# First token tile of a two-layer hybrid trunk: other order, queues and engines for its loads, squares and splits, and the forget columns projected in another chunk

## The chip, the cores and the metric

The kernel runs on one core of one Trainium2 chip. The metric is the device time of one launch in microseconds (us), median of several runs. The core's engines appear in the profile as PE (matmul) and PEld (its weight loads), DVE, ACT, POOL and SP; SP issues DMAs, and so can ACT.

## The reference, cut to what matters

Two layers; in each, an RMS norm, one input projection whose columns go to three token mixers, and an output projection with a second RMS norm and the residual.

```python
h = _rms_norm(x, pre_g)
z = jnp.einsum('bsd,de->bse', h, w_in)          # 2048 x 1024 by 1024 x 3846, float32
a_z, r_z, f_z = jnp.split(z, [A_COLS, A_COLS + R_COLS], axis=-1)
...                                              # a: gelu, spatial gating; r: retention
f_q, f_k, f_v, f_g, f_lg = jnp.split(f_z, [F_WIDTH, 2 * F_WIDTH, 3 * F_WIDTH, 4 * F_WIDTH], axis=-1)
cum_f = jnp.cumsum(jax.nn.log_sigmoid(f_lg + b_f), axis=1)     # 6 forget columns
logits = q k^T * scale + cum_f[q] - cum_f[k]                   # causal softmax, then times v
...
o = jnp.einsum('bse,ed->bsd', y, w_out)
return x + _rms_norm(o, post_g)
```

## The kernel before, in words

Tokens are worked in 16 tiles of 128 (`t`), the 1024 input dimensions in 8 slices of 128 (`k`). Every float32 operand of a large matmul is split into a high part H (an ACT cast to float32r, L175) and a low part L (the difference, on DVE or POOL, L177); a product is three matmuls, H·H, H·L and L·H (L489 to L491 in the chunks that are computed token by token).

`in_proj` takes the 3846 columns in chunks, in this order: `v` (384 value columns and the 6 forget columns, 390 in all), then `g`, `q`, `k` (computed transposed, L266 to L268), then `a0`, `a1` (384 columns each), then `r0`, `r1`, `r2` (512 each). Within a chunk the loop runs over `t`, and within `t` over `k`. At one `k` of tile `t` the operands of tile `t + 1` are split (`token_split`), and `weight_gen` loads and splits the weights of the next chunk. The result `z` of a tile alternates between two PSUM banks.

What follows a tile (`v_post`, `a_post`, `r_post`, `norm`) is a generator on a background list. `bg.add` runs it to its first `yield`; `bg.tick()` after every `k` advances each by one `yield`, and `wait(n)` yields n times. So these numbers are the program's order: every engine executes its instructions in the order in which the code emits them.

`v_post` adds the bias to the 6 forget columns (`lg`, L289). After the last tile of `v` it runs `cum_forget`: Abs, Exp and Ln on ACT, then 16 ticks later a transpose and a running sum (`cs`), 4 ticks later an offset, a split into `cH` and `cL`, and twelve small stores from SP (L322). `r_post` makes `at` (scores times decay, L374) on DVE, which two matmuls read (L379, L380). `e1`, `lt`, `cH`, `cL`, `at` and the `uv` of `a_post` all come from one pool tag with two buffers:

```python
e1 = tp.tile([P, 96], F32, name="e1", tag="at")
cH = tp.tile([96, P], F32R, name="cH", tag="at")
cL = tp.tile([96, P], F32R, name="cL", tag="at")
at = tp.tile([P, 2, P], F32, name="at", tag="at")
```

A tile of this tag can be written once everything that reads the tile two before it is done, DMAs included. DMAs signal on eight lanes in turn, so one is issued once the eighth before it has landed.

At the start of the program 30 transposes of an identity (`warm`, L909) keep PE busy. The first token tile is loaded whole on SP, then the gain, two weight slices, the second token tile, and so on; each weight slice is two DMAs (384 and 6 columns). Its norm is Square on ACT, three small POOL operations, and a product on DVE (`h`, L155); eight transposes go to PSUM (`pt`, L161), a copy to `hT` (L162), and the split from `hT`.

At the end, `last_tile` computes the last 128 tokens' output in two halves of 512 columns, each with a Square, then three POOL operations (L827 to L829), and per half a DVE operation and a store.

Of the kernel before, what the change touches and what calls it, by code (L numbers as in the profile page):

```python
# [12 lines left out]
AF = mybir.ActivationFunctionType  # L13
# [63 lines left out]
def trunk(ctx, tc, a, out):  # L77
# [13 lines left out]
    def U(name, dt=F32):  # L91
        return up.tile([P, 1024], dt, name=name, tag="u")
# [35 lines left out]
    def load_gain(src):  # L128
        t = U("gain")
        nc.sync.dma_start(out=t, in_=src.partition_broadcast(P))  # L130
        return t

    def load_x(src):
        x = U("x")
        nc.sync.dma_start(out=x, in_=src)
        return x
# [64 lines left out]
    def token_half(hT, t, g):  # L201
        return split(hT[t // 4][:, 4 * g:4 * g + 4, (t % 4) * P:(t % 4 + 1) * P])
# [4 lines left out]
    def in_proj(l, hT, w0, cur, next_norm):  # L207
# [1 line left out]
        w_in = a["w_in"][l].rearrange("(k p) e -> k p e", p=P)  # L209
        rz = w_in[:, :, 768:2304].rearrange("k p (c e) -> k p c e", c=4)  # L210
        az = w_in[:, :, 0:768].rearrange("k p (c e) -> k p c e", c=3)
        chunks = [("v", [(w_in[:, :, 3072:3456], 384), (w_in[:, :, 3840:3846], 6)]),
                  ("g", [(w_in[:, :, 3456:3840], 384)]),
                  ("q", [(w_in[:, :, 2304:2688], 384)]), ("k", [(w_in[:, :, 2688:3072], 384)])]
        chunks += [(("a", m), [(az[:, :, :, m * P:(m + 1) * P], 384)]) for m in range(2)]
        chunks += [(("r", m), [(rz[:, :, :, m * P:(m + 1) * P], 512)]) for m in range(3)]
        W = [w0] + [[] for _ in chunks[1:]]

# [77 lines left out]
        def cum_forget():
# [129 lines left out]
        def a_post(m, t, z):  # L426
            s, r = divmod(t, 4)
            if r == 0:
                state["vu"] = U("vu")
            vn, ug = (state["vu"][:, i * 512:(i + 1) * 512].rearrange("p (e r d) -> p e r d", e=2, r=4) for i in range(2))  # L430
            uv = tp.tile([P, 256], F32, name="uv", tag="at")
            nc.scalar.activation(out=uv, in_=z[:, 0:256], func=AF.Gelu_apprx_tanh)
            th = tp.tile([P, P], F32, name="rth", tag="rth")
            nc.scalar.activation(out=th, in_=z[:, 256:384], func=AF.Tanh, scale=0.5)
            g = tp.tile([P, P], F32, name="rg", tag="rg")
            nc.vector.scalar_tensor_tensor(out=g, in0=th, scalar=1.0, in1=z[:, 256:384], op0=ALU.add, op1=ALU.mult)
            nc.gpsimd.tensor_tensor(out=ug[:, :, r], in0=heads(uv[:, 0:P]), in1=heads(g), op=ALU.mult)
            mv = small("mv", [P, 2, 2])
            for e in range(2):
                bs = small("bs", [P, 6])  # L440
                nc.vector.bn_stats(out=bs, in_=uv[:, P + e * HD:P + (e + 1) * HD])
                nc.vector.bn_aggr(out=mv[:, e], in_=bs)
            hr = small("hr", [P, 2])
            nc.gpsimd.tensor_scalar(out=hr, in0=mv[:, :, 1], scalar1=EPS, scalar2=None, op0=ALU.add)
            nc.gpsimd.tensor_tensor(out=hr, in0=hr, in1=mhalf, op=ALU.pow)
            yield from wait(3)
            for e in range(2):
                nc.vector.tensor_scalar(out=vn[:, e, r], in0=uv[:, P + e * HD:P + (e + 1) * HD],
                                        scalar1=mv[:, e, 0:1], scalar2=hr[:, e:e + 1],
                                        op0=ALU.subtract, op1=ALU.mult)  # L450
# [15 lines left out]
            nc.sync.dma_start(out=y[s][0][:, m * P:(m + 1) * P].rearrange("(r p) c -> p r c", p=P),
                              in_=ya.rearrange("p (r c) -> p r c", r=4))
# [3 lines left out]
        for ci in (0, 4, 5, 6, 7, 8):  # L471
# [6 lines left out]
            for t in range(NT):  # L478
# [6 lines left out]
                for k in range(KT):  # L485
                    H, L = cur[k // 4]
                    wH, wL = W[ci][k]
                    c = slice((k % 4) * P, (k % 4 + 1) * P)
                    mm(z[:, :n], lhsT=H[:, c], rhs=wH[:, :n], start=(k == 0), stop=False)  # L489
                    mm(z[:, :n], lhsT=H[:, c], rhs=wL[:, :n], start=False, stop=False)  # L490
                    mm(z[:, :n], lhsT=L[:, c], rhs=wH[:, :n], start=False, stop=(k == KT - 1))  # L491
                    if ci == 0 and t == NT - 1:
                        nxt.append(split(hT[0][:, k]))
                    elif k == (5 if ci == 0 and next_norm else 0) and not (last and t == NT - 1):
                        nxt = token_split(hT, (t + 1) % NT)
                    bg.tick()
                    if last and k % 4 == 3:
                        loads.issue()
                    if fx and k % 2 and fx.chunks < PRE and t >= 10:
                        fx.s_step()  # L500
                        loads.issue()
                        fx.e_step()
                    if last and t == NT - 1 and k in TK:
                        fx.l_step()
                        fx.t_step()
# [267 lines left out]
    def out_proj(l, y, W, og, x_src, x_dst, hT, next_w, ahead):  # L773
# [33 lines left out]
        def last_tile(cur):  # L807
# [8 lines left out]
            for g in range(2):  # L816
                oo = bank("oo", "S")
                for k in range(KT):
# [3 lines left out]
                    for xx, i, first, last in ((H, 0, True, False), (H, 1, False, False), (L, 0, False, True)):  # L822
                        mm(oo, lhsT=xx[:, c], rhs=w[i], start=(k == 0 and first), stop=(k == KT - 1 and last))  # L823
                    bg.tick()
                nc.scalar.activation(out=junk[:, cs[g]], in_=oo, func=AF.Square, accum_out=ss[:, g:g + 1])  # L825
                nc.vector.tensor_tensor(out=o[:, cs[g]], in0=oo, in1=post[:, cs[g]], op=ALU.mult)
            nc.gpsimd.tensor_tensor(out=rs, in0=ss[:, 0:1], in1=ss[:, 1:2], op=ALU.add)  # L827
            nc.gpsimd.tensor_scalar(out=rs, in0=rs, scalar1=1.0 / DM, scalar2=EPS, op0=ALU.mult, op1=ALU.add)  # L828
            nc.gpsimd.tensor_tensor(out=rs, in0=rs, in1=mhalf[:, 0:1], op=ALU.pow)  # L829
            for c in cs:  # L830
                nc.vector.scalar_tensor_tensor(out=o[:, c], in0=o[:, c], scalar=rs, in1=x[:, c], op0=ALU.mult, op1=ALU.add)  # L831
                nc.sync.dma_start(out=x_dst(t)[:, c], in_=o[:, c])

        ys = load_y(0)
        yield
# [41 lines left out]
        if hT is None:  # L877
# [3 lines left out]
    x_src = lambda t: a["x"][t * P:(t + 1) * P, :]  # L881
    hT = [big_tile(f"hT{b}") for b in range(4)]
    W0 = []
    first_w = lambda l: [(a["w_in"][l].rearrange("(k p) e -> k p e", p=P)[:, :, 3072:3456], 384),
                         (a["w_in"][l].rearrange("(k p) e -> k p e", p=P)[:, :, 3840:3846], 6)]
    xq = {}

    def tables_in():
# [14 lines left out]
        if t + 2 < NT:  # L903
            bg.add(norm(xq.pop(t + 2), pg, hT, t + 2, 10, "B"))

    wg = weight_gen(first_w(0), W0, lambda k: k % 3 > 0)
    xq[0] = load_x(x_src(0))
    for _ in range(WU):
        nc.tensor.transpose(bank("warm", "B")[:, 0:P], ident, ident)  # L909
    pg = load_gain(a["pre_gain"][0])  # L910
    next(wg)
    next(wg)
    xq[1] = load_x(x_src(1))
    first = norm(xq.pop(0), pg, hT, 0, 1, "B", (slice(0, 512), slice(512, DM)))
    next(first)
    next(wg)
    next(wg)
    cur = []
    next(first)
    cur.append(token_half(hT, 0, 0))  # L920
    next(first, None)
    bg.add(norm(xq.pop(1), pg, hT, 1, 3, "B"))
    cur.append(token_half(hT, 0, 1))
    next(wg)
    next(wg)
    xq[2] = load_x(x_src(2))
    next(wg)
    next(wg)
    xq[3] = load_x(x_src(3))
    for _ in wg:  # L930
        pass
    for l in range(depth):
        fx, y = in_proj(l, hT, W0, cur, next_norm if l == 0 else None)
        W = []
# [57 lines left out]
```

## Time and profile before

| | us |
|---|---|
| median of 3 runs | 2548.54 (2547.36 to 2549.53) |
| the profiled execution, its own time | 2548.63 |
| its span in the profile | 2546.9 |
| PE busy | 2503.3 (98% of the span) |
| DVE, ACT, POOL busy | 1663.4, 1257.4, 851.3 |

A matmul of the profile is pipelined with the next, so the distance between starts says more than its duration. The chain that ended last is, in its last part, PE without pause and then the tail of the last tile.

### The profile page before, as it was taken

Reading aid. Unit: us, or ns where it says so; the run is one execution under the profiler, and the core shown is the slowest. Engines: PE = TensorE matmul, PEld = TensorE weight load, DVE = VectorE, ACT = ScalarE, POOL = GpSimd, SP = SyncE. Lnnn points to the kernel's source line nnn. Section 1 sums busy time; section 2 is a strip of 40 time slices with the busy share of each in tenths; the row PEclk is TensorE's granted clock in tenths of the full one; section 3 lists DMA queues with packets and bytes.
Section 4 is the critical chain, followed back from the end, with each engine's and each line's share of the span. In section 5 each row is a group of like instructions: output and inputs, shape, how many; then the busy total and the mean of one; then the engine's idle time right before and its main releaser. Section 6 shows DMA issues by size and latency. Waiting matters only on the chain. (4 is left out here: it accounts for less than half of the span.)

```text
span 2546.9 us, 39524 instructions
## 1 busy us (share of the span) xinstructions
PE 2503.3 (98%) x13112; PEld 2138.8 (84%) x13112; DVE 1663.4 (65%) x4173; ACT 1257.4 (49%) x2967; POOL 851.3 (33%) x1372
## 2 busy tenths in 40 slices
PE   9999999999999999999999999999999999999998
PEld 8888899887888888878898889997878888887887
DVE  5544477666668999854454445676666789998433
ACT  7544434333335888843344444433333368888222
POOL 3111267444443333331120113664444323244200
PEclk9999999999999999999999999999999999999999
DMA  6434411101041345253342354111010414542443
GB/s 209 119 91 116 115 46 34 41 14 43 10 109 40 99 109 148 73 183 127 133 134 75 94 121 115 29 38 42 14 38 19 100 47 105 123 134 100 158 149 116
DMA packets 187062, 229.87 MB, mean 90 GB/s; under 512 B 23273, under 2 KB 128681, under 8 KB 185321
## 3 DMA queue, kind: packets, MB, share of 16 engines
q1 hardware_dynamic: 186856, 227.34, 31.8%
q8 instruction: 104, 1.70, 0.3%
q14 instruction: 102, 0.83, 0.1%
HBM read 149.20 MB, written 78.09 MB: 89 GB/s over the span
## 5 line engine op out<-in xcount | busy, mean ns | idle before, releaser
L489 PE MATMUL z<-HL 128*128 128x512 f32 (+2 forms) x1536 | 587.8, 383 | 1.7 <-ACT HL L175 1.7
L491 PE MATMUL z<-HL 128*128 128x512 f32 (+2 forms) x1536 | 561.2, 365 | 3.9 <-DVE HL L177 3.8
L490 PE MATMUL z<-HL 128*128 128x512 f32 (+2 forms) x1536 | 559.7, 364 | 1.8 <-POOL HL L177 1.7
L177 DVE TENSOR_TENSOR HL<-hT,HL 128x512 fp32r<-128x512 f32 x576 | 420.7, 779 | 43.6 <-ACT HL L175 35.0
L865 PE MATMUL oo<-HL 128*128 128x512 f32 x1488 | 355.4, 395 | 0.2
L177 POOL TENSOR_TENSOR HL<-wf,HL 128x512 fp32r<-128x512 f32 (+2 forms) x150 | 178.3, 1195 | 454.7 <-ACT HL L175 280.8
L175 ACT CAST HL<-hT 128x512 fp32r<-128x512 f32 x576 | 324.0, 625 | 0.0
L865 PEld LDWEIGHTS oo<-HL 128*128 128x128 f32 x1488 | 273.3, 188 | 57.8 <-DVE HL L177 1.1
L491 PEld LDWEIGHTS z<-HL 128*128 128x128 f32 x1536 | 288.8, 188 | 38.2 <-DVE HL L177 5.5
L490 PEld LDWEIGHTS z<-HL 128*128 128x128 f32 x1536 | 290.1, 189 | 24.4 <-POOL HL L177 2.4
L489 PEld LDWEIGHTS z<-HL 128*128 128x128 f32 x1536 | 289.8, 189 | 24.1 <-ACT HL L175 2.7
L670 DVE TENSOR_TENSOR PHL<-T,PHL 128x512 fp32r<-128x512 f32 (+3 forms) x402 | 241.4, 604 | 17.5 <-ACT PHL L671 17.4
L671 ACT CAST PHL<-T 128x512 fp32r<-128x512 f32 (+3 forms) x402 | 206.1, 520 | 57.5 <-PE T L659 39.9
L267 PE MATMUL z<-HL 128*128 128x512 f32 x576 | 224.5, 390 | 1.6 <-DVE HL L177 1.5
L266 PE MATMUL z<-HL 128*128 128x512 f32 x576 | 224.6, 390 | 0.0
L268 PE MATMUL z<-HL 128*128 128x512 f32 x576 | 224.1, 389 | 0.0
L612 PE MATMUL S<-kv,q 128*128 128x512 f32 (+1 forms) x480 | 211.0, 442 | 2.3 <-DVE mn L630 2.3
L348 ACT COPY v<-z 128x128 f32<-128x128 f32 x96 | 25.5, 266 | 353.2 <-DVE w L344 353.1
L688 PE MATMUL acc<-PHL,kv 128*128 128x512 f32 x480 | 181.1, 377 | 0.2 <-ACT PHL L671 0.2
L689 PE MATMUL acc<-PHL,kv 128*128 128x512 f32 x480 | 176.5, 368 | 1.5 <-DVE PHL L670 1.0
L646 ACT ACTIVATE row<-row,mn 128x1024 f32<-128x1024 f32 (+2 forms) x192 | 158.2, 824 | 35.8 <-DVE mn L630 35.8
L613 PE MATMUL S<-kL,q 66*128 66x512 f32 (+1 forms) x480 | 175.9, 366 | 0.0
(160 smaller groups left out, 4358.8 us busy)
## 6 DMA issues: line engine op xcount, KB each, us to landing
x<-x SPq DMA_DIRECT2D x48, 512.0 KB
qk<-zHL SPq DMA_DIRECT2D x192, 128.0 KB
wf<-w_in SPq DMA_DIRECT2D x96, 192.0 KB
vscr<-vv SPq DMA_DIRECT2D x32, 384.0 KB
wf<-w_in SPq DMA_DIRECT2D x48, 256.0 KB
kv<-qk SPq DMA_DIRECT2D x24, 512.0 KB
kv<-vscr SPq DMA_DIRECT2D x12, 1024.0 KB
q<-qk SPq DMA_DIRECT2D x48, 256.0 KB
```

Source lines behind the costliest of these rows:

```text
L175: nc.scalar.copy(out=v(H), in_=src)
L177: eng.tensor_tensor(out=v(L), in0=src, in1=v(H), op=ALU.subtract)
L266: mm(z, lhsT=wH[:, c], rhs=H, start=(k == 0), stop=False)
L267: mm(z, lhsT=wH[:, c], rhs=L, start=False, stop=False)
L268: mm(z, lhsT=wL[:, c], rhs=H, start=False, stop=(k == KT - 1))
L489: mm(z[:, :n], lhsT=H[:, c], rhs=wH[:, :n], start=(k == 0), stop=False)
L490: mm(z[:, :n], lhsT=H[:, c], rhs=wL[:, :n], start=False, stop=False)
L491: mm(z[:, :n], lhsT=L[:, c], rhs=wH[:, :n], start=False, stop=(k == KT - 1))
L612: mm(S[:, :n], lhsT=Q[0][:, qc], rhs=K[:, kc], start=True, stop=False)
L670: self.low = lambda: nc.vector.tensor_tensor(out=PL[:, c0:], in0=T[:, c0:], in1=PH[:, c0:], op=ALU.subtract)
L671: nc.scalar.copy(out=PH[:, c0:], in_=T[:, c0:])
L865: mm(oo[g], lhsT=x[:, c], rhs=w[g][i], start=(k == 0 and first), stop=(k == KT - 1 and last))
```

## The change

The first tile's norm and split are written out instead of using `norm` and `weight_gen`; its halves are loaded by SP and ACT, the gain by ACT, all weight slices one after the other by SP; the squares of one half are on DVE; H and L come straight from PSUM, and the copies to `hT` come later. The 6 forget columns move from chunk `v` to `a1` in both layers, and with them `cum_forget`, which is now started inside `a_post` of the last tile of `a1`. In `last_tile` the mean's factor goes into the Square, epsilon into the first half's sum, and the second store to ACT.

```diff
-        chunks = [("v", [(w_in[:, :, 3072:3456], 384), (w_in[:, :, 3840:3846], 6)]),
+        chunks = [("v", [(w_in[:, :, 3072:3456], 384)]),
...
-        chunks += [(("a", m), [(az[:, :, :, m * P:(m + 1) * P], 384)]) for m in range(2)]
+        chunks += [(("a", 0), [(az[:, :, :, 0:P], 384)]),
+                   (("a", 1), [(az[:, :, :, P:2 * P], 384), (w_in[:, :, 3840:3846], 6)])]
...
-            nc.vector.tensor_tensor(out=lg[:, :, t], in0=z[:, 384:390], in1=bf, op=ALU.add)
...
-            if t == NT - 1:
-                yield from cum_forget()
...
             nc.scalar.activation(out=uv, in_=z[:, 0:256], func=AF.Gelu_apprx_tanh)
+            if m == 1:
+                nc.vector.tensor_tensor(out=lg[:, :, t], in0=z[:, 384:390], in1=bf, op=ALU.add)
+                if t == NT - 1:
+                    bg.add(cum_forget())
             th = tp.tile([P, P], F32, name="rth", tag="rth")
...
-                    elif k == (5 if ci == 0 and next_norm else 0) and not (last and t == NT - 1):
+                    elif k == ((5 if t else 6) if ci == 0 and next_norm else 0) and not (last and t == NT - 1):
...
-                nc.scalar.activation(out=junk[:, cs[g]], in_=oo, func=AF.Square, accum_out=ss[:, g:g + 1])
+                nc.scalar.activation(out=junk[:, cs[g]], in_=oo, func=AF.Square, scale=1.0 / 32, accum_out=ss[:, g:g + 1])
+                if g == 0:
+                    nc.gpsimd.tensor_scalar(out=ss[:, 0:1], in0=ss[:, 0:1], scalar1=EPS, scalar2=None, op0=ALU.add)
...
-            nc.gpsimd.tensor_scalar(out=rs, in0=rs, scalar1=1.0 / DM, scalar2=EPS, op0=ALU.mult, op1=ALU.add)
...
-            for c in cs:
+            for c, eng in zip(cs, (nc.sync, nc.scalar)):
...
-                nc.sync.dma_start(out=x_dst(t)[:, c], in_=o[:, c])
+                eng.dma_start(out=x_dst(t)[:, c], in_=o[:, c])
...
+    nc.sync.dma_start(out=x0[:, halves[0]], in_=x_src(0)[:, halves[0]])
+    nc.scalar.dma_start(out=x0[:, halves[1]], in_=x_src(0)[:, halves[1]])
+    pg = U("gain")
+    nc.scalar.dma_start(out=pg, in_=a["pre_gain"][0].partition_broadcast(P))
     for _ in range(WU):
         nc.tensor.transpose(bank("warm", "B")[:, 0:P], ident, ident)
...
+    fs = [w_load(0), w_load(1)]
+    xq[1] = load_x(x_src(1))
+    fs += [w_load(k) for k in range(2, KT)]
...
+    nc.scalar.activation(out=h0[:, halves[0]], in_=x0[:, halves[0]], func=AF.Square, accum_out=ss[:, 0:1])
+    nc.vector.tensor_tensor_reduce(out=h0[:, halves[1]], in0=x0[:, halves[1]], in1=x0[:, halves[1]], scale=1.0, scalar=0.0,
+                                   op0=ALU.mult, op1=ALU.add, accum_out=ss[:, 1:2])
...
+        for k in range(4):
+            kk = 4 * g + k
+            nc.tensor.transpose(pt[:, k * P:(k + 1) * P], h0[:, kk * P:(kk + 1) * P], ident)
+        cur.append(split(pt))
+        pts.append(pt)
+    W0.append(split(fs[2]))
+    W0.append(split(fs[3], on_pool=True))
+    bg.add(norm(xq.pop(1), pg, hT, 1, 5, "B"))
+    W0.append(split(fs[4], on_pool=True))
+    for g in range(2):
+        nc.scalar.copy(out=hT[0][:, 4 * g:4 * g + 4, 0:P], in_=pts[g].rearrange("p (k c) -> p k c", c=P))
+    W0.append(split(fs[5]))
+    W0.append(split(fs[6], on_pool=True))
+    W0.append(split(fs[7]))
```

Line numbers of the rows below are each kernel's own; the changed kernel's stand some lines off (L489 to L491 become L491 to L493, L374 becomes L372).

ACT from the first Square on, before: the square of the first tile, then casts of weights (`wf`) and of tokens, and copies to `hT`, up to the split for the second tile.

```order
L142 ACTIVATE h,ss<-x 128x1024
L175 CAST HL<-wf 128x390 x2
L162 COPY hT_86<-pt 128x4x128
L175 CAST HL<-hT_86 128x512
L162 COPY hT_86<-pt 128x4x128
L142 ACTIVATE h,ss<-x 128x1024
L175 CAST HL<-hT_86 128x512
L175 CAST HL<-wf 128x390 x6
L142 ACTIVATE h,ss<-x 128x1024
L162 COPY hT_86<-pt 128x4x128 x2
L175 CAST HL<-hT_86 128x512 x2
```

The same stretch of ACT in the changed kernel, where L960 is the late copy to `hT`.

```order
L936 ACTIVATE h,ss<-x 128x512
L175 CAST HL<-wf 128x384 x2
L175 CAST HL<-pt 128x512 x2
L175 CAST HL<-wf 128x384 x2
L142 ACTIVATE h,ss<-x 128x1024
L175 CAST HL<-wf 128x384
L960 COPY hT_86<-pt 128x4x128 x2
L175 CAST HL<-wf 128x384 x3
L142 ACTIVATE h,ss<-x 128x1024
L162 COPY hT_86<-pt 128x4x128 x2
L175 CAST HL<-hT_86 128x512 x2
```

The tokens' casts moved ahead of the copies, and six of the eight weight casts now stand behind them. DVE in the changed kernel over the same stretch:

```order
L944 SCALAR_TENSOR_TENSOR h<-x,rs,gain 128x512 x2
L177 TENSOR_TENSOR HL<-pt,HL 128x512 x2
L177 TENSOR_TENSOR HL<-wf,HL 128x384
L155 SCALAR_TENSOR_TENSOR h<-x,rs,gain 128x1024
L177 TENSOR_TENSOR HL<-wf,HL 128x384 x2
L228 MEMSET qbds 128x512
L155 SCALAR_TENSOR_TENSOR h<-x,rs,gain 128x1024
L177 TENSOR_TENSOR HL<-hT_86,HL 128x512 x2
```

The low part of the second token tile (the last row) still stands behind the product for the third tile (the row ahead of it).

ACT before, at the end of `a1`: Gelu and Tanh of its last tile, the casts for tile 1 of `r0`, then the work of `r_post` for tile 0.

```order
L432 ACTIVATE uv<-z 128x256
L434 ACTIVATE rth<-z 128x128
L175 CAST HL<-hT_86 128x512 x2
L348 COPY v<-z 128x128
L350 ACTIVATE rth<-z 128x128
```

The same place in the changed kernel.

```order
L430 ACTIVATE uv<-z 128x256
L297 ACTIVATE e_4471<-lg 128x96
L298 ACT_TABLE_LOAD
L298 ACTIVATE e_4471<-e_4471 128x96
L299 ACT_TABLE_LOAD
L299 ACTIVATE e_4471<-e_4471 128x96
L436 ACT_TABLE_LOAD
L436 ACTIVATE rth<-z 128x128
L175 CAST HL<-hT_86 128x512 x2
```

Three activations on `lg` and three table loads now stand between the Gelu and the Tanh of this tile.

DVE in the changed kernel in tile 2 of `r0`, layer 0, with what each row waits for (DMAHW0 to DMAHW7 are the DMA lanes): the end of `cum_forget`, then the work of `r_post` for tile 1.

```order
L313 TENSOR_SCALAR cs_4598<-cs_4598,off_4648 96x128 [waits Activation_49]
L317 TENSOR_TENSOR cL_4652<-cs_4598,cH_4651 96x128 [waits Activation_49]
L364 TENSOR_TENSOR qd_4674<-pt_4667,qdec_911 128x128 [waits PE_49,Activation_49]
L397 TENSOR_SCALAR yr_4679<-o_4586,mv_4627,hr_4634 128x64 [waits Pool_49]
L397 TENSOR_SCALAR yr_4679<-o_4586,mv_4627,hr_4634 128x64
L372 TENSOR_TENSOR at_4690<-sc_4687,dmat_909 128x256 [waits DMAHW3_49,DMAHW5_49,DMAHW1_49,DMAHW7_49,DVE_49,PE_49]
```

SP at the same place in the changed kernel: the twelve stores, each on the lane that it is shown to wait for.

```order
L320 DMA qk010_235<-cH_4651 16x128 [waits DMAHW7_49,Activation_49]
L320 DMA qk010_235<-cL_4652 16x128 [waits DMAHW0_49,DVE_49]
L320 DMA qk010_235<-cH_4651 16x128 [waits DMAHW1_49]
L320 DMA qk010_235<-cL_4652 16x128 [waits DMAHW2_49]
L320 DMA qk011_236<-cH_4651 16x128 [waits DMAHW3_49]
L320 DMA qk011_236<-cL_4652 16x128 [waits DMAHW4_49]
L320 DMA qk011_236<-cH_4651 16x128 [waits DMAHW5_49]
L320 DMA qk011_236<-cL_4652 16x128 [waits DMAHW6_49]
L320 DMA qk012_237<-cH_4651 16x128 [waits DMAHW7_49]
L320 DMA qk012_237<-cL_4652 16x128 [waits DMAHW0_49]
L320 DMA qk012_237<-cH_4651 16x128 [waits DMAHW1_49]
L320 DMA qk012_237<-cL_4652 16x128 [waits DMAHW2_49]
```

In the kernel before, these stores stand in chunk `g`, and DVE at this place of `r0` has:

```order
L391 BN_AGGR mv_4645<-bs_4649 128x2 [waits DVE_49]
L366 TENSOR_TENSOR qd_4671<-pt_4664,qdec_927 128x128 [waits PE_49,Activation_49]
L399 TENSOR_SCALAR yr_4676<-o_4610,mv_4645,hr_4652 128x64 [waits Pool_49]
L399 TENSOR_SCALAR yr_4676<-o_4610,mv_4645,hr_4652 128x64 [waits DVE_49]
L374 TENSOR_TENSOR at_4687<-sc_4684,dmat_925 128x256 [waits PE_49]
```

The `at` of tile 1, which waited for PE alone, now also waits for lanes 1, 3, 5 and 7, on which the six `cH` stores run.

## Rows read from the trace of the kernel before

**Rows 1.** The page: busy time of PE, its share, instructions

```profile
PE 2503.3 (98%) x13112; PEld 2138.8 (84%) x13112; DVE 1663.4 (65%) x4173; ACT 1257.4 (49%) x2967; POOL 851.3 (33%) x1372
```

**Rows 2.** Timeline, first 22 us: start, duration, engine, line, instruction, idle before

```profile
1.34 6.24 PE L909 MATMUL warm<-ident 128*128 128x128 f32 x30 [1.34 <-POOL ident masks.py:199]
...
4.33 1.06 ACT L142 ACTIVATE h<-x 128x1024 f32<-128x1024 f32 x1 [2.33 <-DMA x<-x]
...
6.43 1.42 DVE L155 SCALAR_TENSOR_TENSOR h<-x,rs,gain 128x512 f32<-128x512 f32 x2 [5.58 <-POOL rs L148]
...
7.38 0.42 PEld L161 LDWEIGHTS pt<-ident,h 128*128 128x128 f32 x4
...
8.86 0.62 ACT L175 CAST HL<-hT 128x512 fp32r<-128x512 f32 x1
...
11.41 1.77 ACT L175 CAST HL<-wf 128x390 fp32r<-128x390 f32 x4
...
19.08 1.28 DVE L155 SCALAR_TENSOR_TENSOR h<-x,rs,gain 128x1024 f32<-128x1024 f32 x1 [1.29 <-POOL rs L148]
...
20.28 1.29 DVE L177 TENSOR_TENSOR HL<-hT,HL 128x512 fp32r<-128x512 f32 x2
21.02 0.45 PE L491 MATMUL z<-HL 128*128 128x390 f32 x1 [0.96 <-DVE HL L177]
```

**Rows 3.** Stretches: busy us (instructions) of PE, PEld, DVE, ACT, POOL; PE clock granted, DMA share, GB/s

```profile
14.00:16.00 2.00, 1.84 (x7) 1.75 (x8) 2.00 (x3) 1.32 (x3) 2.00 (x3) 0.50 1.01 256
16.00:18.00 2.00, 2.00 (x12) 1.90 (x11) 1.74 (x2) 1.63 (x4) 2.00 (x2) 0.72 0.61 248
2542.00:2544.00 2.00, 0.00 (x0) 0.00 (x0) 1.42 (x2) 0.00 (x0) 0.20 (x1) 0.75 0.07 27
```

**Rows 4.** Timeline of ACT where `cum_forget` starts before, end of chunk `v`

```profile
100.74 0.28 ACT L299 ACTIVATE e<-lg 128x96 f32<-128x96 f32 x1 [1.51 <-DVE lg L289]
...
101.36 1.28 ACT L301 ACT_TABLE_LOAD   x1
...
104.25 0.60 ACT L327 ACTIVATE th<-z 128x512 f32<-128x512 f32 x1
```

**Rows 5.** Timeline at the start of `r0`, layer 0

```profile
441.23 0.39 ACT L432 ACTIVATE uv<-z 128x256 f32<-128x256 f32 x1 [2.58 <-POOL hr L445]
441.50 0.27 ACT L434 ACTIVATE rth<-z 128x128 f32<-128x128 f32 x1
441.66 1.14 ACT L175 CAST HL<-hT 128x512 fp32r<-128x512 f32 x2
...
445.17 0.46 POOL L451 TENSOR_TENSOR vu<-vu,ws 128x128 f32<-128x128 f32 x1 [0.66 <-DVE vu L448]
...
447.14 1.02 PE L458 MATMUL sc<-vu,ws 128*128 128x256 f32 x4
```

**Rows 6.** Timeline: the first and a late one of the twelve stores, and a small store and its reader

```profile
113.96 0.32 SPq L322 DMA_DIRECT2D qk<-cH  x1
...
118.50 0.42 SPq L322 DMA_DIRECT2D qk<-cH  x1
...
888.54 0.29 SPq L721 DMA_DIRECT2D rd<-rT  x1
889.76 1.10 SPq L724 DMA_DIRECT2D gy<-rd  x2
```

**Rows 7.** Timeline of tile 2 of `r0`, layer 0

```profile
457.99 0.18 DVE L391 BATCH_NORM_AGGREGATE mv<-bs 128x2 f32<-128x6 f32 x1
...
459.79 0.41 DVE L374 TENSOR_TENSOR at<-sc,dmat 128x256 f32<-128x256 f32 x1
...
461.04 0.33 PE L379 MATMUL o<-v,at 128*128 128x64 f32 x2
```

**Rows 8.** Timeline of the tail: one of the POOL operations after the last matmul

```profile
2541.38 0.19 POOL L828 TENSOR_SCALAR rs<-rs 128x1 f32<-128x1 f32 x1
2541.65 0.54 POOL L829 TENSOR_TENSOR rs<-rs,mhalf 128x1 f32<-128x1 f32 x1
```

More of the change, by code (lines that the diff above doesn't have):

```diff
@@ L883, in trunk @@
     W0 = []
-    first_w = lambda l: [(a["w_in"][l].rearrange("(k p) e -> k p e", p=P)[:, :, 3072:3456], 384),
-                         (a["w_in"][l].rearrange("(k p) e -> k p e", p=P)[:, :, 3840:3846], 6)]
+    first_w = lambda l: [(a["w_in"][l].rearrange("(k p) e -> k p e", p=P)[:, :, 3072:3456], 384)]
     xq = {}
@@ L904, in next_norm @@
             bg.add(norm(xq.pop(t + 2), pg, hT, t + 2, 10, "B"))
-    wg = weight_gen(first_w(0), W0, lambda k: k % 3 > 0)
-    xq[0] = load_x(x_src(0))
+    halves = (slice(0, 512), slice(512, DM))
+    x0 = U("x")
+    nc.sync.dma_start(out=x0[:, halves[0]], in_=x_src(0)[:, halves[0]])
+    nc.scalar.dma_start(out=x0[:, halves[1]], in_=x_src(0)[:, halves[1]])
+    pg = U("gain")
+    nc.scalar.dma_start(out=pg, in_=a["pre_gain"][0].partition_broadcast(P))
     for _ in range(WU):
         nc.tensor.transpose(bank("warm", "B")[:, 0:P], ident, ident)
-    pg = load_gain(a["pre_gain"][0])
@@ L911, in trunk @@
-    next(wg)
-    next(wg)
-    xq[1] = load_x(x_src(1))
[L914 to L917, printed above, removed]
-    cur = []
[L919 to L931, printed above, removed]
+    w_rows = first_w(0)[0][0]
@@ new lines, in trunk, with w_load @@
+    wf = []
+    def w_load(k):
+        if k % 2 == 0:
+            wf.append(U("wf"))
+        f = wf[k // 2][:, (k % 2) * 512:(k % 2) * 512 + 384]
+        nc.sync.dma_start(out=f, in_=w_rows[k])
+        return f
+    fs = [w_load(0), w_load(1)]
+    xq[1] = load_x(x_src(1))
+    fs += [w_load(k) for k in range(2, KT)]
+    xq[2] = load_x(x_src(2))
+    xq[3] = load_x(x_src(3))
+    h0 = U("h")
+    ss = small("ss", [P, 2])
+    rs = small("rs", [P, 1])
+    nc.scalar.activation(out=h0[:, halves[0]], in_=x0[:, halves[0]], func=AF.Square, accum_out=ss[:, 0:1])
@@ new lines, in trunk @@
+    nc.vector.tensor_tensor_reduce(out=h0[:, halves[1]], in0=x0[:, halves[1]], in1=x0[:, halves[1]], scale=1.0, scalar=0.0,
+                                   op0=ALU.mult, op1=ALU.add, accum_out=ss[:, 1:2])
+    nc.gpsimd.tensor_tensor(out=rs, in0=ss[:, 0:1], in1=ss[:, 1:2], op=ALU.add)
+    nc.gpsimd.tensor_scalar(out=rs, in0=rs, scalar1=1.0 / DM, scalar2=EPS, op0=ALU.mult, op1=ALU.add)
+    nc.gpsimd.tensor_tensor(out=rs, in0=rs, in1=mhalf[:, 0:1], op=ALU.pow)
+    W0.append(split(fs[0], on_pool=True))
@@ new lines, in trunk @@
+    for c in halves:
+        nc.vector.scalar_tensor_tensor(out=h0[:, c], in0=x0[:, c], scalar=rs, in1=pg[:, c], op0=ALU.mult, op1=ALU.mult)
+    W0.append(split(fs[1], on_pool=True))
+    cur = []
+    pts = []
+    for g in range(2):
+        pt = bank("pt", "B")
+        for k in range(4):
[4 more added lines that the diff above has]
+    W0.append(split(fs[2]))
@@ L932, in trunk @@
+    W0.append(split(fs[3], on_pool=True))
+    bg.add(norm(xq.pop(1), pg, hT, 1, 5, "B"))
+    W0.append(split(fs[4], on_pool=True))
+    for g in range(2):
+        nc.scalar.copy(out=hT[0][:, 4 * g:4 * g + 4, 0:P], in_=pts[g].rearrange("p (k c) -> p k c", c=P))
+    W0.append(split(fs[5]))
+    W0.append(split(fs[6], on_pool=True))
+    W0.append(split(fs[7]))
     for l in range(depth):
```

## The prediction, made before the changed kernel ran

> **What bounds the kernel now.** I read the page first: PE is busy 98% of the span [rows 1]. So time is gained only where PE waits, and nearly every new wait of PE is lost time. Then the timeline of the first 22 us, because the change starts there. The reader is to see a chain that hands on from engine to engine: Square on ACT at 4.33, the product `h` on DVE at 6.43, transposes at 7.38, the cast of the first tokens at 8.86, four weight casts at 11.41, and only at 21.02 the third matmul of the second tile, behind a low part on DVE [rows 2]. From there PE runs without a pause worth the name. Third, the places to which `cum_forget` moves: the start of `r0`, where PE, ACT and POOL meet [rows 5], and tile 2 of `r0` [rows 7]. Prices of `cum_forget` itself come from chunk `g`, where it ran so far [rows 4, 6].
>
> **The start: a gain of 3.1 us.** The first transposes can't move forward. PE executes 30 warm-up transposes first, from 1.34 to 7.58 by their row, and `h` was at work at 6.43 [rows 2]; an earlier `h` finds PE occupied. What is saved is behind them. The first four transposes end at 7.80; the cast, now straight from PSUM, starts at about 7.9 instead of 8.86. From there I sum ACT in its new order up to the first cast for tile 1. Distances of starts are 0.42 for a weight cast (four take 1.77, one of them 0.52: 1.25 over three) and 0.52 for a token cast (two take 1.14, one 0.62) [rows 2, 5]. That the single cast takes 0.52 is an estimate from 0.62 for 512 columns. A copy to `hT` is taken as 0.55, between these, and a Square as its 1.06. Two token casts, six weight casts, two Squares and four copies make 1.04 + 2.52 + 2.12 + 2.20 = 7.9 us, so the cast for tile 1 starts near 15.8 and ends at 16.4. DVE is later: the Square of the third tile ends near 14.7, POOL's two operations take about 0.9 (0.19 and 0.54 in [rows 8], and hops), the product 1.28 [rows 2], to 17.0, and the low part half of 1.29. With hops, the third matmul of tile 1 comes at 17.9 against 21.02: 3.1 us. The bounds: the weights' low parts on POOL and DVE may hold tile 0 longer, which leaves 1 us; and if ACT and DVE weave better, 5 us. The square on DVE has no row. It costs at least the 0.65 of a low part and at most the 1.28 of a product over twice the columns, and in either case ends before PE is done with the warm-up, so it is priced at nothing; without the warm-up it would cost up to 0.6. Loading by two queues is likewise covered.
>
> **The tail: 0.27 us.** One POOL operation after the last Square disappears: the distance from 2541.38 to 2541.65 [rows 8]. Its replacement is done while PE computes the second half. The second store waits for DVE in either queue, so its move is worth nothing.
>
> **The columns: nothing.** Six columns leave 384 matmuls of `v` and join 384 of `a1`, in both layers.
>
> **The first new wait, at the start of `r0`: 3.7 us in each layer.** In the last tile of `a1` the Tanh started at 441.50, while the Gelu's row ends at 441.62 [rows 5]. Now the bias on DVE, Abs, Exp, Ln and three table loads stand between. Before, Abs to the next Tanh took 104.25 - 100.74 = 3.51 us with two loads [rows 4]; a third load of 1.28 makes 4.8. With the bias on DVE, the Tanh starts at about 441.87 + 4.80 = 446.67: 5.17 us later. Behind it in ACT's queue are the casts for tile 1, on DVE the gate and the norm's statistics, then POOL, whose last step (L451) is what PE's spatial matmul reads. That step ended at 445.63 while PE came at 447.14 [rows 5]: 1.5 us of cover. Moved by 5.17 it ends at 450.80, so PE waits 3.7 us there. The low parts for tile 1 hold PE too, for about 1.6 us of the same time (the casts move from 441.66 to 446.83, one cast and one low part end at 448.4, PE wanted it at about 446.9). The bounds are 1.6, if the spatial matmul is found ready after all, and 4.2. The old place gives nothing back: PE ran on there.
>
> In the trace the activations run back to back with their loads: Abs to Tanh, 3.51 us, leaves no room beside two loads of 1.28 and three activations of 0.28 (3.40) [rows 4]. The Trainium skill, ScalarE: Activation LUTs, What ACT_TABLE_LOAD costs, gives the load the same 1283 ns but adds a drain of about 1380 ns to every switch of tables; by that rule, an estimate from the page, three switches would make this wait some 4 us longer in each layer. The rows speak against it.
>
> **The second new wait, in tile 2 of `r0`: 4.1 us in each layer, and more for the clock.** `at` of tile 1 takes the buffer of `cH`, and six DMAs read `cH`. The order shows DVE waiting for their lanes there, where only PE was waited for. In tile 2 DVE is busy until 458.17 [rows 7]; the offset, the cast `cH` and the hops take about 0.7 (0.28 for such an activation, [rows 4]), so the first store is issued at 458.85. The last `cH` store is the eleventh of twelve; before, it was issued 118.50 - 113.96 = 4.54 us after the first [rows 6], here at 463.4. A small store and the DMA that reads its result start 1.22 us apart [rows 6], so it lands at 464.6. Then `at` takes 0.41, and L379 on PE, which was at 461.04 [rows 7], comes at 465.1: 4.1 us. All in times of the profile before; the first wait moves everything alike. Behind `at` on DVE are the state update and the work for tile 2; PE can't pass L379 in its own queue. The `cL` stores that hold the next `at` land half a microsecond later and a tile ahead of it. Bounds: 3.4 if the stores land at once, 5.0 if other traffic delays them.
>
> A pause of PE can cost clock. After PE's waits in the first tile the granted clock was 0.50 (1.2 GHz) from 14 to 16 us and on average 0.72 to 18, that is, the lower level until about 17.1, some 3 us of work at half pace: 1.5 us lost. And in the tail, with PE done, it is 0.75 from 2542 to 2544 [rows 3]. I take 1.4 us per layer behind the second wait, none behind the first, in which PE still does some matmuls; the bounds are nothing and 1.5 for each of four waits.
>
> **The sum.** -3.1 - 0.3 + 2 x 3.7 + 2 x 4.1 + 2 x 1.4 = +14.8. The profiled execution took 2548.63, which is 0.09 over the median, so the forecast is 2548.5 + 14.8 = 2563.3 us.
>
> **The rivals.**
> - The second wait is covered: the stores of `cH` land before `at` is wanted. It decides at 460.6, L379's time less `at`: the six stores would have to land within 1.8 us of the first issue. For it, other DMAs of the stretch are few. Against it, the spacing of the issues, 0.45 each. Without this wait and its clock the sum is -3.4 + 7.4 = +4.0, 2552.5 us, which is not slower by what can be told.
> - The table loads are mostly covered, because the spatial matmul's input comes in time and only the low part holds PE: two times 1.6 in place of 3.7, 2559.1. For it, the cover of 1.5 us; against it, DVE's order, in which the statistics follow the Tanh's gate.
> - The start gives nothing and the clock falls at all four waits: 2548.5 - 0.3 + 7.4 + 8.2 + 6 = 2569.8. For it, the warm-up that ends where it ended; against it, the casts that move.
> - ACT pauses at each switch of tables here, for as long as a load: three times 1.28 [rows 4] per layer, 2563.3 + 7.7 = 2571.0. Rows 4 speak against it. The page named above would have such a pause.
> - Both new waits are covered and the start gives its full 5 us: 2543.2. For it, that before `cum_forget` cost PE nothing; against it, both reasons above.
>
> **How the numbers follow.** The forecast with its bounds gets 0.60, the covered loads 0.13, the deeper case 0.10, the pause at the switches 0.02, the covered second wait 0.10, both covered 0.05. The forecast's own range runs from 2556 to 2569, by the bounds of its terms taken partly together. To leave out no more than 2 in 10, the range is 2551 to 2570. About 0.2% (5 us) is what a measurement of this kernel can tell from no change: faster 0.05, the same 0.11 (the covered second wait and a little of the covered loads), slower 0.84.
>
> **What would show it.** In the profile after: the third matmul of tile 1 near 17.9; three table loads in a row on ACT at the end of `a1`, and PE idle some 3.7 us ahead of the spatial matmul, released by POOL's L453 (the old L451); in tile 2 of `r0`, DVE's `at` released by a DMA that reads `cH`, PE idle some 4 us ahead of the two matmuls on `at`, and a granted clock under 1 behind it; all of it in both layers. Wrong would be: `at` on time, a spatial matmul that PE doesn't wait for, or a first tile that saves 6 us or more.

## The result and the profile after

| | before | after |
|---|---|---|
| median | 2548.11 us (2547.36 to 2549.53, 4 runs) | 2583.91 us (2583.34 to 2584.43, 4 runs) |
| ratio, 95% interval | | 1.0138 (1.0126 to 1.015) |

The change costs 35.8 us, where 14.8 was forecast. The direction was right, the time lies 14 us above the range. The page of the kernel after, beside [rows 1]:

```profile
span 2582.3 us, 39530 instructions
PE 2516.4 (97%) x13112; PEld 2146.4 (83%) x13112; DVE 1667.6 (65%) x4175; ACT 1261.9 (49%) x2967; POOL 856.5 (33%) x1373
```

The span grew by 35.4 us [rows 1]: PE's busy time by 13.1, for the same 13112 instructions, its pauses by 22.3. That the same work keeps PE longer goes with the lower clock shown below; the mean granted clock of the execution is 0.993, against 0.999 before. The pauses are in the waits of PE (after; what PE waited with and for, us in total, times, longest):

```profile
PE sc L460 <- POOL vu L453: 15.6, 10, 2.4
PE o L377 <- DVE at L372: 6.9, 2, 3.5
...
PE sc L367 <- ACT qbds L362: 3.2, 4, 1.5
...
PE pt L952 <- DVE h L944: 2.6, 2, 1.8
```

The first group was there before, with less:

```profile
PE sc L458 <- POOL vu L451: 6.8, 8, 1.1
```

The second is new and stands where the prediction put it; the third (in tile 2 of `r0`) and the fourth (at the start) were in no step of it. To see where the loss grows, I took the same matmul in both traces and subtracted the starts. Layer 0: -1.18 at the first matmul of chunk `a1`, 4.79 at the first matmul of `r0` (445.77 against 440.98), 8.54 at the spatial matmul of [rows 5], 9.98 once the clock is back and 10.27 ahead of the waits of tile 2, 15.62 at the first matmul on `at` of [rows 7], 18.37 once the clock is back again. Layer 1 goes from 15.88 at its `a1` to 20.19 at its `r0`, 25.96 ahead of the waits of tile 2 and 34.23 behind them. Of the growth in `a1`, 5.97 and 4.31, some 1.1 each are the wider matmuls, which experiment 1 leaves standing; `v` gives about as much back. So three places of each layer make the loss, and one of them, `a1`, is not in the prediction.

**In `a1`.** ACT's Tanh of the gate in four tiles, after:

```profile
395.39 0.28 ACT L436 ACTIVATE rth<-z 128x128 f32<-128x128 f32 x1 [0.23 <-DVE lg L432]
400.24 0.28 ACT L436 ACTIVATE rth<-z 128x128 f32<-128x128 f32 x1 [0.81 <-DVE lg L432]
405.09 0.28 ACT L436 ACTIVATE rth<-z 128x128 f32<-128x128 f32 x1 [1.40 <-DVE lg L432]
409.90 0.28 ACT L436 ACTIVATE rth<-z 128x128 f32<-128x128 f32 x1 [1.94 <-DVE lg L432]
```

Before, the Tanh waited for nothing but its Gelu, and came once per tile of PE, 4.17 apart:

```profile
399.62 0.27 ACT L434 ACTIVATE rth<-z 128x128 f32<-128x128 f32 x1
403.79 0.27 ACT L434 ACTIVATE rth<-z 128x128 f32<-128x128 f32 x1
```

After, the Tanhs are 4.85 apart, while 24 matmuls of 0.178 make a tile of 4.27 on PE. The wait grows by 0.58 per tile. A group of four tiles later, layer 0, after:

```profile
427.25 0.28 ACT L436 ACTIVATE rth<-z 128x128 f32<-128x128 f32 x1 [1.39 <-DVE lg L432]
...
427.56 0.29 DVE L438 SCALAR_TENSOR_TENSOR rg<-rth,z 128x128 f32<-128x128 f32 x1 [0.35 <-ACT rth L436]
...
429.44 1.00 POOL L447 TENSOR_TENSOR hr<-hr,mhalf 128x2 f32<-128x2 f32 x1
...
430.42 1.25 POOL L177 TENSOR_TENSOR HL<-wf,HL 128x512 fp32r<-128x512 f32 x1
430.48 1.47 DVE L450 TENSOR_SCALAR vu<-uv,mv,hr 128x64 f32<-128x64 f32 x2 [0.60 <-POOL hr L447]
431.87 0.16 DVE L432 TENSOR_TENSOR lg<-z,bf 128x6 f32<-128x6 f32 x1
432.03 0.46 POOL L453 TENSOR_TENSOR vu<-vu,ws 128x128 f32<-128x128 f32 x1 [0.36 <-DVE lg L432]
432.06 0.28 ACT L436 ACTIVATE rth<-z 128x128 f32<-128x128 f32 x1 [1.93 <-DVE lg L432]
...
432.54 1.13 PE L460 MATMUL sc<-vu,ws 128*128 128x256 f32 x4 [2.36 <-POOL vu L453]
```

It is a loop: Tanh, gate, statistics, POOL's `hr`, DVE's `vu`, and then the 0.16 us bias `lg` of the next tile, which the next Tanh waits for. One turn takes 4.81 here, with `vu` at 1.47 beside a weight's low part on POOL (0.54 at 445.44, where POOL has none). The bias closed this loop; before, no Tanh waited for DVE. After three tiles the cover is used up and PE waits 2.36 for the spatial matmul.

**At the start of `r0`**, after, beside [rows 5]:

```profile
446.03 0.39 ACT L430 ACTIVATE uv<-z 128x256 f32<-128x256 f32 x1 [2.34 <-PE z L493]
...
446.71 0.29 ACT L297 ACTIVATE e<-lg 128x96 f32<-128x96 f32 x1 [0.30 <-DVE lg L432]
...
447.01 1.28 ACT L298 ACT_TABLE_LOAD   x1
...
448.61 1.28 ACT L299 ACT_TABLE_LOAD   x1
...
450.20 1.28 ACT L436 ACT_TABLE_LOAD   x1
...
451.50 0.28 ACT L436 ACTIVATE rth<-z 128x128 f32<-128x128 f32 x1
...
455.17 0.46 POOL L453 TENSOR_TENSOR vu<-vu,ws 128x128 f32<-128x128 f32 x1 [0.65 <-DVE vu L450]
...
455.68 2.07 PE L460 MATMUL sc<-vu,ws 128*128 128x256 f32 x4 [1.77 <-POOL vu L453]
```

Gelu to Tanh grew from 0.27 to 5.47, and the spatial matmul came 8.54 - 4.79 = 3.75 later. The 1.77 shown is the last of three waits of PE there; ahead of it stand 0.92 for a token cast on ACT (at 452.33) and 0.34 for a low part on DVE (at 453.41).

**Tile 2 of `r0`**, after, beside [rows 6, 7]:

```profile
470.02 0.32 SPq L320 DMA_DIRECT2D qk<-cH  x1
...
470.65 0.70 PE L367 MATMUL sc<-qbds,kT 128*128 128x256 f32 x2 [1.43 <-ACT qbds L362]
...
474.56 0.42 SPq L320 DMA_DIRECT2D qk<-cH  x1
...
476.19 0.42 DVE L372 TENSOR_TENSOR at<-sc,dmat 128x256 f32<-128x256 f32 x1 [4.76 <-DMA qk<-cH]
...
476.66 0.69 PE L377 MATMUL o<-v,at 128*128 128x64 f32 x2 [3.48 <-DVE at L372]
```

Two waits stand here: 1.43 for a copy on ACT that queues behind the cast of `cH` (469.70 to 470.00), and 3.48 for `at`, which is released by the eleventh store.

**The clock**, after, the columns of [rows 3]: the start, `a1`, behind the first wait, behind the second.

```profile
16.00:18.00 2.00, 1.84 (x7) 1.50 (x7) 1.95 (x3) 1.23 (x3) 1.83 (x3) 0.50 0.00 0
...
410.00:412.00 2.00, 1.62 (x5) 1.33 (x6) 1.67 (x7) 1.72 (x4) 1.51 (x3) 0.68 0.00 0
412.00:414.00 2.00, 2.00 (x8) 2.00 (x7) 2.00 (x4) 0.00 (x0) 1.92 (x2) 0.50 0.00 0
414.00:416.00 2.00, 2.00 (x13) 2.00 (x12) 0.61 (x2) 0.00 (x0) 0.80 (x2) 0.97 0.84 216
...
456.00:458.00 2.00, 2.00 (x6) 1.54 (x6) 1.46 (x3) 1.31 (x4) 1.70 (x3) 0.50 0.04 8
458.00:460.00 2.00, 2.00 (x9) 1.63 (x8) 1.11 (x3) 0.00 (x0) 0.00 (x0) 0.87 0.00 0
...
476.00:478.00 2.00, 1.34 (x5) 1.34 (x6) 1.65 (x5) 0.05 (x1) 0.00 (x0) 0.50 0.52 108
478.00:480.00 2.00, 2.00 (x6) 1.52 (x6) 1.35 (x3) 1.42 (x4) 1.80 (x3) 0.50 0.21 63
480.00:482.00 2.00, 2.00 (x7) 1.52 (x6) 1.06 (x5) 0.00 (x0) 0.70 (x2) 0.50 0.00 0
482.00:484.00 2.00, 2.00 (x11) 1.60 (x10) 0.16 (x1) 0.68 (x3) 0.19 (x1) 0.90 0.00 0
```

Behind the first wait PE works at 1.2 GHz from 455.68 to about 458.5, behind the second from 476.66 to about 482.4: half of 2.8 and of 5.7 is lost, 1.4 and 2.9. In `a1` the three rows at 0.68, 0.50 and 0.97 make a loss of 1.7, in layer 0 only; that is the difference between 5.97 and 4.31. These losses are this trace's. In the trace of experiment 2, where the code of `a1` and of the first wait is the same, layer 0 of `a1` stays at 1.00, layer 1 falls (0.50 from 1686 to 1688), and behind the first wait of layer 0 the clock is at 0.50 from 454 to 460 and costs 2.9 where it costs 1.4 here.

**The start**, after, beside [rows 2]:

```profile
1.35 5.32 PE L916 MATMUL warm<-ident 128*128 128x128 f32 x30 [1.35 <-POOL ident masks.py:199]
...
4.62 0.69 DVE L937 CUSTOM_DVE_ANT_0 h<-x 128x512 f32<-128x512 f32 x1 [3.77 <-DMA x<-x]
...
7.07 2.71 DVE L944 SCALAR_TENSOR_TENSOR h<-x,rs,gain 128x512 f32<-128x512 f32 x2 [1.75 <-DMA gain<-pre_gain]
...
8.48 0.63 PE L952 MATMUL pt<-ident,h 128*128 128x128 f32 x4 [1.81 <-DVE h L944]
...
14.19 2.01 DVE L155 SCALAR_TENSOR_TENSOR h<-x,rs,gain 128x1024 f32<-128x1024 f32 x1 [1.83 <-POOL rs L148]
...
15.18 0.69 PE L492 MATMUL z<-HL 128*128 128x384 f32 x1 [1.09 <-POOL HL L177]
...
21.69 0.34 PE L493 MATMUL z<-HL 128*128 128x384 f32 x1
```

The third matmul of tile 1 stands at 21.69, against 21.02 before. `h` waited for the gain, PE for `h`, and PE was free from 6.67 on. One execution says little here: in the profiles of experiments 1, 2, 5 and 6, with the same start, this matmul stands at 20.44, 21.95, 20.45 and 20.56, PE's first wait for `h` is 0.85 to 1.51, and the warm-up ends between 7.0 and 7.5. Its 30 transposes are the same in all: they start 0.21 apart and then 0.11 to 0.14, from 4.6 on here and from 6.9 on before.

### The profile page after: what moved, and what is told of

It reads as the page before. It is cut to its first block, busy times and chain, and to the rows that moved or that the text cites. A ratio compares the mean times of both kernels' runs of the same rounds, so it can differ in the third digit from the quotient of the medians.

```text
span 2582.3 us, 39530 instructions
## 1 busy us (share of the span) xinstructions
PE 2516.4 (97%) x13112; PEld 2146.4 (83%) x13112; DVE 1667.6 (65%) x4175; ACT 1261.9 (49%) x2967; POOL 856.5 (33%) x1373
## 5 line engine op out<-in xcount | busy, mean ns | idle before, releaser
L491 PE MATMUL z<-HL 128*128 128x512 f32 (+2 forms) x1536 | 591.4, 385 | 2.7 <-ACT HL L175 2.7
L493 PE MATMUL z<-HL 128*128 128x512 f32 (+2 forms) x1536 | 564.2, 367 | 3.6 <-DVE HL L177 3.6
L493 PEld LDWEIGHTS z<-HL 128*128 128x128 f32 x1536 | 290.6, 189 | 37.9 <-DVE HL L177 5.4
L491 PEld LDWEIGHTS z<-HL 128*128 128x128 f32 x1536 | 292.3, 190 | 26.4 <-ACT HL L175 4.6
```

## The experiments

Each is the kernel after with one edit, where nothing else is said. Every ratio is to the kernel before on the same chip. A ratio is taken from paired rounds and can differ a little from the quotient of the medians. The difference of two ratios is uncertain by about 0.002 (5 us) where it is taken to after, and by 0.0013 (3 us) between two of 6 to 10. So the places are also compared in the traces, by the starts of the same matmuls. With the first four kernels before was at 2547.55 us, with the next four at 2548.22, with the last two at 2548.01.

**1. The bias moved behind the gate** in tiles 0 to 14 of `a1` (`lg_late`):

```diff
-            if m == 1:
+            if m == 1 and t == NT - 1:
                 nc.vector.tensor_tensor(out=lg[:, :, t], in0=z[:, 384:390], in1=bf, op=ALU.add)
...
             nc.vector.scalar_tensor_tensor(out=g, in0=th, scalar=1.0, in1=z[:, 256:384], op0=ALU.add, op1=ALU.mult)
+            if m == 1 and t < NT - 1:
+                nc.vector.tensor_tensor(out=lg[:, :, t], in0=z[:, 384:390], in1=bf, op=ALU.add)
```

> The changed kernel, with the bias on the forget columns moved behind the Tanh's gate on DVE in tiles 0 to 14 of a1 (tile 15 as it was). Theory: in a1 the Tanh waits for this bias, the bias waits in DVE's queue behind the previous tile's normalisation and that behind POOL, and the spatial matmul is late by this chain; of the 5 us that a1 loses in each layer about 1.3 are columns and the rest is this, so the kernel takes some 7 to 8 us less than the changed one, about 2576. Rival: a1 loses by its wider matmuls and its sixteen weight loads in place of eight; then the move changes nothing, 2584.

Measured: 2571.90 us, 1.0101 (1.0085 to 1.0117), 0.0037 less than after, or 9.4 us, more than forecast. In the waits of PE of this kernel the spatial matmul falls to

```profile
PE sc L461 <- POOL vu L454: 9.7, 10, 1.8
```

and its Tanhs are 4.27 apart, PE's own pace, though `vu` takes 1.50 beside POOL here too. By the traces `a1` grows by 2.2 us in both layers together, against 10.3 after: 8.1. So the order of one 0.16 us instruction is worth 4 to 5 us per layer, with the low clock of layer 0 in it.

**2. Own buffers for `cH` and `cL`** (`own_buffers`):

```diff
-            cH = tp.tile([96, P], F32R, name="cH", tag="at")
-            cL = tp.tile([96, P], F32R, name="cL", tag="at")
+            cH = tp.tile([96, P], F32R, name="cH", tag="cH", bufs=1)
+            cL = tp.tile([96, P], F32R, name="cL", tag="cL", bufs=1)
```

> The changed kernel, with cH and cL in buffers of their own instead of the pair that at uses. Theory: at of tile 1 no longer waits for the six stores; the pause of PE ahead of the two matmuls on at goes, 3.8 us in each layer, and the low clock behind it, 2.8 us; the 1.6 us wait for the copies to kT and qbds stays. About 13 us less than the changed kernel, 2571. Rival: the clock falls anyway, because of the earlier waits in the same stretch, and PE loses part of the time at the next step; then 7 us less, 2577.

Measured: 2569.96 us, 1.0089 (1.0074 to 1.0104), 0.0049 less, or 12.5 us. The wait for `at` is gone from the waits of PE and the granted clock is 1.00 from 476 to 484 us. The wait for the copies stays, 3.3 us in all. By the traces tile 2 of `r0` gives back 12.9 in both layers.

**3. Only the forget columns moved**: the kernel before with the first part of the diff (`forget_only`).

> The kernel before, with only the forget columns and cum_forget moved to a1 as in the change; start and tail as before. Theory: the whole loss hangs on this move and the new start gives nothing, so this is within 2 us of the changed kernel, 2582 to 2585. Rival: the new start gains some 3 us that the forget columns hide; then this is slower than the changed kernel by 3, 2587.

Measured: 2583.74 us, 1.0142 (1.0125 to 1.0159), against 1.0138 for after. Within the interval the whole loss is in this move.

**4. Only start and tail changed**: the forget columns and `cum_forget` back in `v` (`start_tail_only`).

> The changed kernel, with the forget columns and cum_forget back in v as before (the first tile's weights then come in sixteen DMAs in place of eight); the new start and tail stay. Theory: within 2 us of the kernel before, 2547 to 2550. Rival: the new start is worth 3 us when cum_forget is out of the way, 2545.

Measured: 2545.90 us, 0.9994 (0.9985 to 1.0004). Not told apart from before; the time lies between the theory and the rival. In its trace the granted clock is 1.00 in all stretches from 8 to 24 us and the third matmul of tile 1 stands at 20.01, 1.0 ahead of before.

**5. `cum_forget` starts one tick later**, so that its table loads stand behind the Tanh and the casts (`forget_start_late`):

```diff
         def cum_forget():
+            yield
...
-            yield from wait(16)
+            yield from wait(15)
```

> The changed kernel, with the three activations of cum_forget and their table loads one tick later, behind the Tanh of the last a1 tile and the casts for tile 1 of r0 (the rest of cum_forget at its old ticks). Theory: the wait at the start of r0 is these loads ahead of the Tanh; behind the casts ACT has 4 us with nothing due, so the wait of 4.5 to 5 us in each layer goes, and the kernel takes 2574 to 2575. Rival: the third load, now ahead of the Tanh of r_post, makes tile 2 of r0 late in its place; then 3 us of it come back in each layer, 2580.

Measured: 2573.34 us, 1.0097 (1.0083 to 1.011), 0.0041 less, or 10.4 us. By the traces the start of `r0` gives back 9.1 in both layers; 1.1 in each is left.

**6. All three repairs** (1 in all tiles, 2 and 5), with the changed start and tail (`forget_fixed`).

> All three repairs at once on the changed kernel: own buffers for cH and cL, the bias behind the gate in every a1 tile, cum_forget's activations one tick later; start and tail as changed. Theory: the three losses add, 12 + 13 + 9.5 less what they share, and the kernel is back at 2547 to 2551, as the kernel before, with the copies' wait of some 1.5 us in each layer left over. Rival: the losses overlap in such a way that one wait takes the place of another, and the sum falls short by 5 us or more, 2556.

Measured: 2552.33 us, 1.0015 (1.0006 to 1.0024). The time is 1 us above the forecast. The three add up: 0.0037 + 0.0049 + 0.0041 = 0.0127, measured together 0.0123, closer than the intervals can bear out.

**7. The gain first**: 6, with the gain loaded in halves on both queues ahead of the weights, and the low parts of the first two weight slices on DVE behind `h` (`forget_fixed_gain_first`):

```diff
-    nc.scalar.dma_start(out=pg, in_=a["pre_gain"][0].partition_broadcast(P))
+    for c, eng in zip(halves, (nc.sync, nc.scalar)):
+        eng.dma_start(out=pg[:, c], in_=a["pre_gain"][0][c].partition_broadcast(P))
...
-    W0.append(split(fs[0], on_pool=True))
...
-    W0.append(split(fs[1], on_pool=True))
+    W0.append(split(fs[0]))
+    W0.append(split(fs[1]))
```

> As forget_fixed, and in the start the gain in halves on SP and ACT ahead of the weight slices, and the low parts of the first two weight slices on DVE behind h in place of POOL. Theory: the new start gives nothing because h waits for the gain (7.07 in the changed kernel, with POOL done at 6.59) and its second half stands beside POOL's low parts (2.71 us for two halves that took 1.42 before); with both out of the way the first matmul comes near 8.8 instead of 10.3, and the kernel is 1 to 2 us under forget_fixed. Rival: what bounds the first two tiles is the later chain over ACT; then the same as forget_fixed.

Measured: 2549.79 us, 1.0011 (1.0002 to 1.0019), 2.5 us below 6, which the intervals don't tell apart. Its timeline:

```profile
6.59 1.42 DVE L945 SCALAR_TENSOR_TENSOR h<-x,rs,gain 128x512 f32<-128x512 f32 x2 [1.46 <-DMA gain<-pre_gain]
...
7.49 1.29 PE L954 MATMUL pt<-ident,h 128*128 128x128 f32 x8 [0.43 <-DVE h L945]
...
18.39 0.59 ACT L162 COPY hT<-pt 128x512 f32<-128x512 f32 x1 [1.84 <-PE pt L161]
18.87 1.14 ACT L175 CAST HL<-hT 128x512 fp32r<-128x512 f32 x2
```

The first transposes come 1 us sooner than in the kernel after, but tile 1's cast stands at 18.87, not at 15.8 as forecast: ACT waits for PE's transposes there, not PE for ACT.

**8. The start of before**, the forget columns moved and repaired as in 6, the changed tail (`forget_fixed_old_start`).

> The start of the kernel before, with the forget columns moved and repaired as in forget_fixed, and the changed tail. Theory: the new start is worth about 0 to 1.5 us, so this is that much above forget_fixed. Rival: the new start costs 0.7 us, as the first profile of the changed kernel read; then that much below.

Measured: 2551.85 us, 1.0015 (1.0006 to 1.0024), the same ratio as 6: the changed start as such is worth nothing that can be measured.

**9. The end of `cum_forget` three ticks later**: 7, with the last wait of 4 ticks made 7, so that its cast leaves the copies alone (`all_repairs`).

> As forget_fixed_gain_first, with the last piece of cum_forget (offset, cH, cL, stores) three ticks later in tile 2 of r0, behind the copies to kT and qbds. Theory: what is left of the loss are two waits of the score matmuls for these copies, 1.5 us in each layer; they go, and the kernel is at 0.9995 to 1.0000 of the kernel before, about 3 us under forget_fixed_gain_first. Rival: cL stands ahead of at's successors on DVE and something else becomes late by the same time; then 1.001 as forget_fixed_gain_first.

Measured: 2547.46 us, 1.0000 (0.9991 to 1.0009), 0.0011 or 2.8 us less than 7. The intervals overlap, but PE's wait for the copies falls from 3.3 us to 0.4 in all, and by the traces tile 2 gives back 2.7. Experiment 10, which differs from this one in that the columns and `cum_forget` stay in `v`, is at 0.9990: what the repaired move costs is not told from nothing.

**10. The start of 7 alone**, the forget columns in `v` as before, the changed tail (`start_gain_first`).

> The forget columns and cum_forget in v as in the kernel before, the changed tail, and the start of forget_fixed_gain_first (gain ahead of the weights, low parts of two slices on DVE). Theory: the new start with an early gain is worth some 1.5 to 2 us over the kernel before, 0.9990 to 0.9994, and this beats both kernels. Rival: the sixteen weight DMAs of the first chunk make the later slices late and take it back; then 1.0000.

Measured: 2546.58 us, 0.9990 (0.9981 to 0.9999): the one kernel that beats before, by a margin that its interval barely bears.

## Why the prediction was right and wrong

| us, both layers | forecast | measured |
|---|---|---|
| start and tail | -3.4 | not told from 0 (experiment 4) |
| bias in `a1` | none | 9.4 (experiment 1) |
| first wait, with its clock | 7.4 + 0 | 10.4 (experiment 5) |
| second wait, with its clock | 8.2 + 2.8 | 12.5 (experiment 2) |
| copies behind the cast of `cH` | none | 2.8 (7 against 9) |

The last four make 35.1 of the 35.8. That they close so well is luck, as each is uncertain by 3 to 5 us. By the traces the same four places give 8.1, 9.1, 12.9 and 2.7, together 32.8, and the 2.2 left at the start of `r0` in experiment 5. The sum on record is off by itself: its terms make +15.0, not +14.8, and 2563.5 us.

- **"The columns: nothing"** is the step that failed. As widths they do cancel. But the columns bring the bias with them, and I counted it once, in the last tile, where `cum_forget` starts. It runs in all 16 tiles, between Gelu and Tanh, and its place in DVE's queue closed the loop shown above, which cost 9.4 us (8.1 by the traces) where nothing was taken. The step to take was: for an instruction put ahead of another engine's work, name what stands before it in its own queue.
- **The start, "an earlier `h` finds PE occupied"**: failed. The warm-up ended at 6.67 where 7.58 was taken over from before (that differs between executions of the same start), the gain landed for `h` at 7.07, and PE waited 1.81 (0.85 to 1.51 in the other profiles with this start). Behind that, the sum of ACT's work was the wrong bound. PE's transposes for tile 1 stand behind the matmuls of tile 0, these waited for weights' low parts on POOL (1.09 at 15.18), DVE's product took 2.01 in place of 1.28, and the clock was at 0.50 by then. The text had the low parts as a bound that "leaves 1 us"; they left nothing. Experiment 7 shows that the gain was not the whole cause, and experiment 4 that the clock was not: at 1.00 the matmul stands at 20.01, 1.0 gained and not 3.1.
- **The first wait**: right in place, releaser and size. The Tanh came 5.2 later than its Gelu's pace allows, forecast 5.17, and the spatial matmul 3.75 later, forecast 3.7. The clock behind it was mis-sized: none was taken, 1.4 per layer was lost in the trace after. With this and some small waits, up to tile 2 the layers lose 5.5 and 5.8 there; experiment 5 takes away 10.4 (9.1 by the traces).
- **The loads of tables**: Abs to Tanh is 4.79 in the trace after, with three loads of 1.28, each starting as the activation ahead of it ends, forecast 4.80. The drain of about 1380 ns per switch of the Trainium skill, ScalarE: Activation LUTs, What ACT_TABLE_LOAD costs, does not show here; the rival is out.
- **The second wait**: mechanism right. The eleventh store was issued 4.54 after the first, to the digit what [rows 6] gave. It landed and released `at` 1.63 after its issue, not 1.22, and the first store came 0.9 later than worked out (470.02, against 458.85 + 10.27). So PE came 15.62 - 10.27 = 5.35 later, not 4.1. Of this, 1.6 would have been there without `at`: the copies for L367, which I had not looked at though the cast of `cH` is put ahead of them on ACT. The clock behind it was mis-sized too, 2.9 for 1.4 per layer (in layer 0 of experiments 1, 3 and 5 it is 1.7).
- **The tail**: the last Square started at 2540.33 before and 2576.00 after, the last products at 2542.23 and 2577.68. That is 1.90 and 1.68, a gain of 0.22 for the forecast 0.27.
- **The deeper rival** (2569.8) had the start and the clock nearly right. What it and the range lacked was the wait in `a1`.

Open: at the end of layer 1's softmax mixer, where PE waits for DVE, the traces differ for no reason that I found: against before, after loses 1.3 us there, `start_tail_only` 3.5, `own_buffers` nothing. Why the clock falls in layer 0 of `a1` in one trace and in layer 1 in another is not known either; the pause in `a1` is some 3.2 us in each layer, the clock 1.7 where it falls.

## What to carry to other kernels

A small instruction costs its place, not its length: ahead of every engine that will wait for it, ask what stands before it in its own queue, in every iteration and not only in the one where the diff does something special. Where a chain of engines runs once per tile, add up one whole turn and compare it with PE's time for a tile; a turn that is 0.6 us too long is invisible for three tiles and then a pause. To a new pause of PE of 2 to 3.5 us belongs its clock, which here cost another 1.4 to 2.9 us, not the same in every trace of the same place; price it as a range.

## What was not expected of the hardware

- DVE and POOL slow each other. The product on 128x1024 took 2.01 us with POOL's low parts beside it and 1.28 without [rows 2]; two on 128x512 took 2.71 in the changed start and 1.42 again in experiment 7, where POOL's low parts were moved to DVE behind them; the two `vu` operations 1.47 beside a low part. In experiment 4 `h` started ahead of POOL: it took 1.41, and POOL's two low parts 2.55, where they took 0.99 and 1.00 in the changed kernel.

```profile
7.02 1.41 DVE L945 SCALAR_TENSOR_TENSOR h<-x,rs,gain 128x512 f32<-128x512 f32 x2 [1.79 <-DMA gain<-pre_gain]
...
7.75 2.55 POOL L177 TENSOR_TENSOR HL<-wf,HL 128x390 fp32r<-128x390 f32 x2 [1.25 <-ACT HL L175]
```

- The granted clock stayed at 0.50 for 2.8 us behind the first wait and 5.7 us behind the second, though PE worked without pause from the first matmul on in both. Behind the same first wait it stayed there from 454 to 460 in experiment 2.
